# Key norms from the diagonal of (Gram matrix times decays), once per layer, and another PSUM bank for one unit

## The chip, the cores and the metric

The kernel runs on one core of a Trainium2 chip. The metric is device time in microseconds (us) for one execution; lower is better. Engines are named as in the profile: PE is TensorE (matmuls; PEld its weight loads), DVE is VectorE, ACT is ScalarE, POOL is GpSimd, and SP issues the DMAs. The times are a median of three runs; the profile is of one execution.

## The reference, cut to what matters

Two identical layers run on x, 512 tokens by 1024 features. In each, one projection feeds a gated DeltaNet branch (8 heads of 128) and a sliding-window attention branch (16 query heads of 64); both are merged, projected, and an MLP follows. Everything is float32. Of the DeltaNet branch the change concerns this:

```python
def l2norm(t):
    return t * lax.rsqrt(jnp.sum(t * t, axis=-1, keepdims=True) + EPS)      # EPS = 1e-6

k = l2norm(k.reshape(B, S, 8, 128)); beta = jax.nn.sigmoid(b_in); g = cumsum(g) in a chunk
decay = where(causal, exp(g[..., :, None] - g[..., None, :]), 0)
L = where(strict, einsum('bhnid,bhnjd->bhnij', k * beta[..., None], k) * decay, 0)
u = triangular_solve(L, v * beta[..., None], lower=True, unit_diagonal=True)
w = triangular_solve(L, k * beta[..., None] * exp(g)[..., None], lower=True, unit_diagonal=True)
a_intra = einsum('bhnid,bhnjd->bhnij', q, k) * decay
k_dec = k * exp(g_last - g)[..., None]
# then a scan over the chunks with the state S
```

So each key needs its squared norm (plus EPS): the inverse square root scales values, its inverse times beta scales the matrix that is solved, the intra-chunk products and the decayed keys. The decay matrix has ones on its diagonal.

## The kernel before, in words

**Weights and big matmuls.** PE is almost wholly taken up by weight matmuls. A float32 weight chunk of 128x1024 (`wr`, loaded by SP into 5 rotating buffers) is split into a high part `wh` (a cast on ACT, L323) and the rest `wl` (a subtraction on DVE, L324), up to 4 chunks ahead of PE. A chunk gives 24 matmuls of 128x512 output (`h_h,wh`, `h_l,wh`, `h_h,wl`; L339 to L341). The Tile scheduler orders the instructions of each engine from the program's dependences and its own estimates, except where the program fixes an order (`Order`, `keep_in_program_order`); an edit can therefore move work that it does not name.

**PSUM banks.** `PM` gives 2 banks for results of big matmuls (`ps_kp`, `ps_gb`, `ps_zp`, `ps_us` and so on), `PS` 3 banks for smaller results (`ps_s`, `ps_pt`, `ps_o`, `ps_gt`), `PK` one bank (Gram matrices `ps_a`, later `ps_i`), `PZ` two.

**Decays.** `decays()` transposes the cumulative log decays `gc` (128x32: partition = place in the chunk, column = head and chunk) on PE (`ps_gt`, L683), stores them in DRAM (`gd`) and broadcasts them into a 128x512 matrix `D` per head, which goes to DRAM (`dd`).

**The K stage** (16 rounds of the list `MIX`, about 80 to 190 us of the span in layer 1 and 986 to 1096 us in layer 2). Each round mixes big-matmul units (`gb_unit`: a merge gate; `ga_early`; `k_unit`: one head's keys) with one attention group of 128 queries by 4 heads. An attention group goes: scores `ps_s` on PE (L892, L893); mask add into `M`, maximum `nm`, `es`, and denominator `den` on DVE (L896 to L913); exponential and scaling of `M` on ACT (scaling L916); transposes `ps_pt` of `M` on PE (L922, bound to wait for L916); on DVE and POOL the high and low parts `pf_h`, `pf_l` (L412, POOL's mask `pc` L932); `ps_o` on PE (L938); the result into `qt` (L942).

`k_unit(h)` takes a key projection `ps_kp` through convolution and SiLU on DVE and ACT (`kk`, L714 to L718), loads `D`, and computes four 128x128 Gram matrices into `ps_a` (L735). Then DVE reads that bank twice: four operations with the identity (L740) that also sum each row into `ssk` (the squared norms), EPS (L742), the inverse root `irk` on POOL (L744), reciprocal (L747), times beta into `cj` (L748), and four operations that write `uu` = Gram times `cj` times `D` (L752). `uu` goes to DRAM (`ud`, L754).

**The solve.** From MIX's last rounds on, `solve()` runs in steps (`steps(n)` in the code) on DVE beside other units. It loads the 128 diagonal blocks of 32x32 (8 heads of 16) from `ud` into `ub`, one block per partition (L783); 31 steps of a product and a sum (L798, L801) invert them into `pb`; the result goes through DRAM (`pd`, L804) to `Tc` and, transposed, `Pc`.

**The V, Z and attention-output stages** follow: `ps_qp`, `ps_vp`, `ps_zp` units, and at about 246 us the loop over `ps_us` (attention output; takes the split attention results `oT_h`, `oT_l`; evacuated by L1214 into `mb`). `d_load` (L993) loads the matrix of a head (`ur`) from `ud`; `d_inverse` builds 128-wide inverses from `ur`, `Tc`, `Pc` with small matmuls `ps_i` (L1013, L1018), whose operands `T`, `Pt` POOL clears and copies (L1048); `d_turn` makes `kds` from `cj`; `d_chain` scales by `cj` and `irk` (`aT` L1155, `vs` and `kd` L1162).

## Time and profile before

| what | us |
|---|---|
| median of 3 runs | 1830.95 (1829.16 to 1831.1) |
| the profiled execution's own time | 1830.59 |
| span of that execution's profile | 1828.6 |
| PE busy, share of the span | 1809.1, 99% |
| PE weight loads (PEld) busy | 1503.9, 82% |
| DVE busy | 1292.1, 71% |
| ACT busy | 940.9, 51% |
| POOL busy | 211.2, 12% |
| mean granted TensorE clock | 0.999 |

A profile line of a group reads: line, engine, operation, output<-input by the program's names, shapes, count | busy us in total, mean ns of one | idle us of the engine ahead of them, and what ended most of it. A line of the timeline reads: start in us, duration, engine, line, operation, shapes, and in square brackets the engine's idle time just before and what ended it (the releaser). A line of the waits reads: who waits for whom: us in total, times, longest. "x4" at a timeline line means four in a row, with their common duration. Starts of consecutive big matmuls lie 0.22 to 0.23 us apart although each lasts 0.39 us: they are pipelined. DVE is busy 91% of the time in the K stage, against 71% over the span.

### The profile page before, as it was taken

The numbers are of one execution on the slowest core, as the hardware profiler recorded it, in microseconds if no ns is written. First come the engines' busy times: TensorE is split into PE (matmuls) and PEld (weight loads), VectorE is DVE, ScalarE is ACT, GpSimd is POOL, SyncE is SP. The second block draws the span as 40 slices with busy tenths as digits, with TensorE's granted clock in tenths as the row PEclk, the third lists the DMA queues.
The fourth block names the chain that finished last, engine by engine and source line by source line (L and its number), as shares of the span: only waits on it lengthen the run. The fifth ranks groups of instructions, "written<-read, shape, count | busy, mean of one in ns | idle before, by whom it ended". The sixth has DMA issues, their size and how long they took to land.

```text
span 1828.6 us, 26748 instructions
## 1 busy us (share of the span) xinstructions
PE 1809.1 (99%) x9598; PEld 1503.9 (82%) x9598; DVE 1292.1 (71%) x2466; ACT 940.9 (51%) x1913; POOL 211.2 (12%) x386
## 2 busy tenths in 40 slices
PE   9999999999999999999999999999999999999998
PEld 8888778888788888888898887888887898888886
DVE  5499796887566758684556997968885568585934
ACT  6678742444434645544347877234444346554442
POOL 0322102221101000000003221022111010000000
PEclk9999999999999999999999999999999999999999
DMA  5633447554453363564245343485545534544631
GB/s 188 202 118 116 115 149 223 179 170 149 124 191 124 96 216 120 168 217 151 93 151 181 104 127 110 167 234 165 160 139 153 172 119 135 174 163 148 233 102 46
DMA packets 146422, 278.48 MB, mean 152 GB/s; under 512 B 33569, under 2 KB 66657, under 8 KB 146290
## 3 DMA queue, kind: packets, MB, share of 16 engines
q1 hardware_dynamic: 145778, 276.75, 47.4%
q8 instruction: 75, 1.23, 0.3%
q14 instruction: 57, 0.47, 0.1%
q0 software_dynamic: 512, 0.03, 0.0%
HBM read 239.38 MB, written 37.36 MB: 151 GB/s over the span
## 4 chain that ended last, share of the span: by engine, by line
PE 84%; DVE 6%; ACT 5%; DMA 3%; issue 1%; POOL 1%; SPq 0%; POOLq 0%; DVEq 0%; ACTq 0%
PE ps_f L340 6%; PE ps_f L339 6%; PE ps_f L341 6%; PE ps_p L402 3%; PE ps_p L404 3%; PE ps_p L400 3%; PE ps_b L388 3%; PE ps_b L387 3%; PE ps_b L389 3%; PE ps_vp L339 2%; PE ps_us L339 2%; PE ps_ud L339 2%; PE ps_vp L341 2%; PE ps_ud L341 2%; PE ps_ud L340 2%; PE ps_us L340 2%
## 5 line engine op out<-in xcount | busy, mean ns | idle before, releaser
L323 ACT CAST wh<-wr 128x1024 fp32r<-128x1024 f32 (+1 forms) x332 | 343.1, 1040 | 542.2 <-PE ps_f L340 145.8
L324 DVE TENSOR_TENSOR wl<-wr,wh 128x1024 fp32r<-128x1024 f32 (+1 forms) x332 | 400.4, 1216 | 303.6 <-ACT wh L323 300.6
L339 PE MATMUL ps_f<-g_h,wh 128*128 128x512 f32 x448 | 174.3, 389 | 0.0
L340 PE MATMUL ps_f<-g_l,wh 128*128 128x512 f32 x448 | 174.3, 389 | 0.0
L341 PE MATMUL ps_f<-g_h,wl 128*128 128x512 f32 x448 | 174.3, 389 | 0.0
L402 PE MATMUL ps_p<-wl,P_h 128*128 128x512 f32 x336 | 131.4, 391 | 0.4 <-DVE wl L324 0.3
L404 PE MATMUL ps_p<-wh,P_l 128*128 128x512 f32 x336 | 130.8, 389 | 0.0
L400 PE MATMUL ps_p<-wh,P_h 128*128 128x512 f32 x336 | 129.5, 389 | 0.0
L437 POOL TENSOR_TENSOR pr<-pq,pw 128x1 f32<-128x1 f32 x16 | 9.8, 613 | 807.6 <-DVE pq L436 807.6
L339 PEld LDWEIGHTS ps_f<-g_h,wh 128*128 128x128 f32 x448 | 84.1, 188 | 17.4
L341 PEld LDWEIGHTS ps_f<-g_h,wl 128*128 128x128 f32 x448 | 84.1, 188 | 17.4
L340 PEld LDWEIGHTS ps_f<-g_l,wh 128*128 128x128 f32 x448 | 84.1, 188 | 17.4
L402 PEld LDWEIGHTS ps_p<-wl,P_h 128*128 128x128 f32 x336 | 63.1, 188 | 15.8 <-DVE wl L324 2.4
L400 PEld LDWEIGHTS ps_p<-wh,P_h 128*128 128x128 f32 x336 | 63.1, 188 | 13.3
L404 PEld LDWEIGHTS ps_p<-wh,P_l 128*128 128x128 f32 x336 | 63.1, 188 | 12.8
L387 PE MATMUL ps_b<-wh,h_h 128*128 128x432 f32 (+1 forms) x192 | 71.1, 370 | 0.0
L388 PE MATMUL ps_b<-wl,h_h 128*128 128x432 f32 (+1 forms) x192 | 70.5, 367 | 0.3 <-DVE wl L324 0.3
L389 PE MATMUL ps_b<-wh,h_l 128*128 128x432 f32 (+1 forms) x192 | 70.2, 366 | 0.0
L293 DVE TENSOR_TENSOR wr<-wr 128x1024 f32<-128x1024 f32 x48 | 58.0, 1220 | 2.6 <-DMA wr<-in_weights_dram 1.9
L340 PE MATMUL ps_qp<-h_l,wh 128*128 128x512 f32 x128 | 54.0, 422 | 0.0
L339 PE MATMUL ps_vp<-h_h,wh 128*128 128x512 f32 x128 | 53.9, 421 | 0.0
L341 PE MATMUL ps_vp<-h_h,wl 128*128 128x512 f32 x128 | 53.6, 419 | 0.0
(359 smaller groups left out, 4873.6 us busy)
## 6 DMA issues: line engine op xcount, KB each, us to landing
wr<-in_weights_dram SPq DMA_DIRECT2D x320, 512.0 KB, 3.5
wr<-in_weights_dram SPq DMA_DIRECT2D x24, 432.0 KB, 3.6
D<-dd SPq DMA_DIRECT2D x32, 256.0 KB, 3.2
xd<-xo SPq DMA_DIRECT2D x12, 512.0 KB, 2.8
xt<-xd SPq DMA_DIRECT2D x24, 256.0 KB, 3.7
D<-gd SPq DMA_DIRECT2D x16, 256.0 KB, 6.5
dd<-D SPq DMA_DIRECT2D x16, 256.0 KB, 3.9
kkd<-kk SPq DMA_DIRECT2D x16, 256.0 KB, 2.0
```

Of the source, the lines that this page charges most:

```text
L293: tt(out=held[j], in0=held[j], in1=part(i, k, j), op=ALU.add)
L323: nc.scalar.copy(wh[:, :w], wr[:, :w])
L324: sub(out=wl[:, :w], in0=wr[:, :w], in1=wh[:, :w].bitcast(F32), op=ALU.subtract)
L339: mm(ps, lhsT=wh[:, k, :], rhs=hi, start=k == 0, stop=False)
L340: mm(ps, lhsT=wh[:, k, :], rhs=lo, start=False, stop=False)
L341: mm(ps, lhsT=wl[:, k, :], rhs=hi, start=False, stop=k == KT - 1)
L387: mm(pss[t], lhsT=hi[:, tsl], rhs=wh[:, r, :], start=k == 0, stop=False)
L388: mm(pss[t], lhsT=hi[:, tsl], rhs=wl[:, r, :], start=False, stop=False)
L389: mm(pss[t], lhsT=lo[:, tsl], rhs=wh[:, r, :], start=False, stop=k == KT - 1)
L400: mm(pss[t], lhsT=hi[:, c], rhs=wh[:, r, :], start=first, stop=False, skip_group_check=onto)
L402: mm(pss[t], lhsT=hi[:, c], rhs=wl[:, r, :], start=False, stop=False, skip_group_check=onto)
L404: mm(pss[t], lhsT=lo[:, c], rhs=wh[:, r, :], start=False, stop=last, skip_group_check=onto)
```

## The change

`k_unit` reads the Gram bank once: `uu` = Gram times `D` in a single 128x512 product (L741 after), without norms. Since `D`'s diagonal is one, the squared norms stand on the diagonal of `uu`. `solve()` reads them from the diagonals of all its blocks at once: `ssq` = diagonal of `ub` plus EPS (L782, 128x32), sent to DRAM (`nd`), reciprocal, times beta in block layout (`bq`, loaded from the new `bd`), and one 128x1024 product scales `ub` (L786). `nd` comes back as `nT` (32x128); behind the last step a PE transpose `ps_nt` brings the norms to token layout, from which one reciprocal and one product make `cj` for all heads and POOL makes `irk` in one 128x32 power. `d_load` now scales `ur`, which is loaded unscaled, by `cj`: 4 activations of 128x128 per head on ACT. The transpose `ps_gt` carries beta along (64 columns rather than 32). And the first `ps_us` unit takes a bank of `PS` rather than `PM`.

Line numbers after the change are 2 to 8 higher (L323 becomes L325, L324 L326, L735 L739, L892 L897, L916 L921, L922 L927, L1214 L1222).

```diff
-        beta = s1("beta", 32)
+        gcb = s1("gcb", 64)
+        gc, beta = gcb[:, 0:32], gcb[:, 32:64]
...
             ps = PS("ps_gt")
-            tr(ps[:32, :P], gc, ident)
-            gT = sm.tile([32, P], F32, name="gT", bufs=1)
-            nc.vector.tensor_copy(gT, ps[:32, :P])
-            dma(gd, gT)
+            tr(ps[:64, :P], gcb, ident)
+            gT = sm.tile([64, P], F32, name="gT", bufs=1)
+            nc.vector.tensor_copy(gT, ps[:64, :P])
+            dma(gd, gT[0:32])
+            dma(bd, gT[32:64])
...
-        cj, irk = [], []
+        irk, cj = s1("irk", 32), s1("cj", 32)
...
             u_ = T[5]("uu")
-            sk_ = sm.tile([P, NC], F32, name="ssk")
-            for c in range(NC):
-                sl = slice(c * P, (c + 1) * P)
-                stt(out=u_[:, sl], in0=ps[:, sl], scalar=1.0, in1=ident, op0=ALU.mult,
-                    op1=ALU.mult, accum_out=sk_[:, c:c + 1])
-            ts(out=sk_, in0=sk_, scalar1=EPS, scalar2=None, op0=ALU.add)
-            ir = sm.tile([P, NC], F32, name="irk", bufs=H + 1)
-            ptt(out=ir, in0=sk_, in1=phalf, op=ALU.pow)
-            irk.append(ir)
-            cc = sm.tile([P, NC], F32, name="cj", bufs=H + 1)
-            nc.vector.reciprocal(cc, sk_)
-            tt(out=cc, in0=cc, in1=hc(beta)[:, h, :], op=ALU.mult)
-            cj.append(cc)
-            for c in range(NC):
-                sl = slice(c * P, (c + 1) * P)
-                stt(out=u_[:, sl], in0=ps[:, sl], scalar=cc[:, c:c + 1], in1=d[:, sl],
-                    op0=ALU.mult, op1=ALU.mult)
+            tt(out=u_, in0=ps, in1=d, op=ALU.mult)
             dma(umat(h), c4(u_))
...
+            bq = s1("bq", 32)
+            dma(bq, bd.rearrange("g (b j) -> (g b) j", b=4))
             pb = X4("pb")
...
             uv = ub.rearrange("p (j i) -> p j i", j=32)
+            sq = s1("ssq", 32)
+            ts(out=sq, in0=ub[:, 0:1024:33], scalar1=EPS, scalar2=None, op0=ALU.add)
+            dma(nd.rearrange("g (b j) -> (g b) j", b=4), sq)
+            nc.vector.reciprocal(sq, sq)
+            tt(out=sq, in0=sq, in1=bq, op=ALU.mult)
+            tt(out=uv, in0=uv, in1=sq.unsqueeze(2).broadcast_to([P, 32, 32]), op=ALU.mult)
+            nT = sm.tile([64, P], F32, name="gT", bufs=1)
+            dma(nT[0:32], nd)
...
+            ps = PS("ps_nt")
+            tr(ps[:, 0:32], nT[0:32], ident[:32, :32])
+            nc.vector.tensor_copy(irk, ps[:, 0:32])
+            nc.vector.reciprocal(cj, irk)
+            tt(out=cj, in0=cj, in1=beta, op=ALU.mult)
+            ptt(out=hc(irk), in0=hc(irk), in1=phalf.unsqueeze(1).broadcast_to([P, H, NC]), op=ALU.pow)
             dma(pd, pb)
...
                     dma(uview(h), umat(h))
+                    for c in range(NC):
+                        act(out=uview(h)[:, c, :], in_=uview(h)[:, c, :], func=AF.Copy,
+                            scale=cj[:, h * NC + c:h * NC + c + 1])
...
         for m in range(KT):
-            ps = PM("ps_us")
+            ps = (PM if m else PS)("ps_us")
```

(`d_turn` and `d_chain` take their columns from the two new tiles.) Instructions in the whole program: PE 8748 to 8750, DVE 2404 to 2258, ACT 1723 to 1787, POOL 391 to 377, SP 836 to 844.

The diff moves more than it names. PE's order stays the same outside the K stages, but there small blocks stand up to 16 big matmuls earlier: among the transposes `ps_pt` of layer 1, the third stands behind 402 big matmuls rather than 407, the tenth behind 572 rather than 585, the thirteenth behind 658 rather than 674, the last three where they were. PE, layer 1, where the second head's Gram matrices come, before:

```order
L340 MATMUL ps_gb<-h_l,wh 128x512
L341 MATMUL ps_gb<-h_h,wl 128x512
L892 MATMUL ps_s<-kT_h,qT 128x128
L735 MATMUL ps_a<-kk 128x128 x4
L938 MATMUL ps_o<-pf_l,vp 128x512
L893 MATMUL ps_s<-kT_l,qT 128x128
L892 MATMUL ps_s<-kT_h,qT 128x128
L893 MATMUL ps_s<-kT_l,qT 128x128
```

PE, the same place, after:

```order
L342 MATMUL ps_gb<-h_l,wh 128x512
L343 MATMUL ps_gb<-h_h,wl 128x512
L943 MATMUL ps_o<-pf_l,vp 128x512
L739 MATMUL ps_a<-kk 128x128 x4
L897 MATMUL ps_s<-kT_h,qT 128x128
L898 MATMUL ps_s<-kT_l,qT 128x128
L897 MATMUL ps_s<-kT_h,qT 128x128
L898 MATMUL ps_s<-kT_l,qT 128x128
```

The second half of one attention group (`ps_o`) now stands ahead of the Gram matrices, and all score matmuls of the next stand behind them.

DVE, about the first two heads of layer 1, before (`kk` and `qT` belong to key convolution and query layout):

```order
L747 RECIPROCAL cj<-ssk 128x4
L866 SCALAR_TENSOR_TENSOR qT<-ps_q,qT 64x512
L718 SCALAR_TENSOR_TENSOR kk<-th,kk 128x512
L748 TENSOR_TENSOR cj<-cj,beta 128x4
L896 TENSOR_TENSOR M<-ps_s,ban 128x256
L752 SCALAR_TENSOR_TENSOR uu<-ps_a,cj,D 128x128 x4
L896 TENSOR_TENSOR M<-ps_s,ban 128x256
L412 TENSOR_TENSOR pf_l<-ps_pt,pf_h 128x512
L904 TENSOR_REDUCE nm<-M 128x4
```

DVE, the same place, after:

```order
L871 SCALAR_TENSOR_TENSOR qT<-ps_q,qT 64x512
L718 SCALAR_TENSOR_TENSOR kk<-ps_kp,cw,kk 128x511
L901 TENSOR_TENSOR M<-ps_s,ban 128x256 x2
L722 SCALAR_TENSOR_TENSOR kk<-th,kk 128x512
L909 TENSOR_REDUCE nm<-M 128x4
L414 TENSOR_TENSOR pf_l<-ps_pt,pf_h 128x512
L910 TENSOR_TENSOR nm<-nm,nsk 128x4
L912 TENSOR_TENSOR es<-nm,nsk 128x4
L326 TENSOR_TENSOR wl<-wr,wh 128x1024
L741 TENSOR_TENSOR uu<-ps_a,D 128x512
```

The norm chain between the mask adds is gone; one product stands behind the next `wl`.

DVE at the start of the solve, layer 1, before (`oT_l` are split attention results):

```order
L324 TENSOR_TENSOR wl<-wr,wh 128x1024
L904 TENSOR_REDUCE nm<-M 128x4
L942 TENSOR_TENSOR qt_421<-ps_o,qt_421 64x512
L905 TENSOR_TENSOR nm<-nm,nsk 128x4
L412 TENSOR_TENSOR oT_l<-qt_419,oT_h 128x128
L907 TENSOR_TENSOR es<-nm,nsk 128x4
L412 TENSOR_TENSOR oT_l<-qt_420,oT_h 128x128
L324 TENSOR_TENSOR wl<-wr,wh 128x1024
L798 TENSOR_TENSOR tmp<-ub,pb 128x1
```

DVE, the same place, after:

```order
L912 TENSOR_TENSOR es<-nm,nsk 128x4
L782 TENSOR_SCALAR ssq<-ub 128x32
L414 TENSOR_TENSOR oT_l<-qt_421,oT_h 128x128
L414 TENSOR_TENSOR oT_l<-qt_422,oT_h 128x128
L917 TENSOR_TENSOR den<-den,es 128x4
L918 RECIPROCAL den<-den 128x4
L414 TENSOR_TENSOR oT_l<-qt_423,oT_h 128x128
L784 RECIPROCAL ssq<-ssq 128x32
L785 TENSOR_TENSOR ssq<-ssq,bq 128x32
L786 TENSOR_TENSOR ub<-ub,ssq 128x1024
L326 TENSOR_TENSOR wl<-wr,wh 128x1024
L797 TENSOR_TENSOR tmp<-ub,pb 128x1
```

The first read of `ub` (L782) now stands ahead of a softmax denominator (`den`), where the first step's product used to stand behind it.

ACT, behind the Z stage of layer 1, before:

```order
L1103 ACTIVATE sz<-ps_zp 128x512
L1111 ACTIVATE wq<-qq 128x512
L323 CAST wh<-wr 128x1024 x9
L772 ACTIVATE sga<-ps_ga 128x512
L323 CAST wh<-wr 128x1024
L772 ACTIVATE sga<-ps_ga 128x512
L1162 ACTIVATE vs<-kvx,irk 128x128
```

ACT, the same place, after:

```order
L325 CAST wh<-wr 128x1024
L1119 ACTIVATE wq<-qq 128x512
L325 CAST wh<-wr 128x1024 x7
L1000 ACTIVATE ur<-ur,cj 128x128 x15
L325 CAST wh<-wr 128x1024
L760 ACTIVATE sga<-ps_ga 128x512
L1000 ACTIVATE ur<-ur,cj 128x128
L325 CAST wh<-wr 128x1024
```

Fifteen scalings of `ur` stand between two casts; eight more come for heads 4 and 5 behind a later convolution, then four and two and two.

## The prediction

> **What bounds the kernel now.** I began with the engines' shares on the page, then took the K stages apart by windows, then asked what PE waited for in them, and last read the timeline around each wait.

> ```profile
> span 1828.6 us, 26748 instructions
> ...
> PE 1809.1 (99%) x9598; PEld 1503.9 (82%) x9598; DVE 1292.1 (71%) x2466; ACT 940.9 (51%) x1913; POOL 211.2 (12%) x386
> ```

> PE is busy in all but 1828.6 - 1809.1 = 19.5 us. A matmul's record overlaps the next one, so this alone proves little; but the starts of big matmuls below lie 0.22 to 0.23 us apart, one after another. Now the stretches that the change touches (K stage of layer 1, its end, K stage of layer 2):

> ```profile
> core 0: us, PE busy (x) PEld busy (x) DVE busy (x) ACT busy (x) POOL busy (x), PEclk, DMA share, GB/s
> 80.00:190.00 110.00, 108.14 (x573) 88.08 (x571) 100.03 (x296) 86.85 (x257) 26.78 (x46) 1.00 0.36 115
> 190.00:246.00 56.00, 55.30 (x263) 44.11 (x262) 44.53 (x122) 41.21 (x123) 7.55 (x12) 1.00 0.36 101
> 986.00:1096.00 110.00, 107.79 (x575) 88.23 (x573) 99.61 (x296) 86.52 (x257) 26.69 (x46) 1.00 0.36 115
> ```

> DVE is busy for 100.03 of 110 us, and still PE stands idle for only 110 - 108.14 = 1.9 us of them. What PE waited for from 80 to 250 us:

> ```profile
> PE ps_pt L922 <- ACT M L916: 2.0, 3, 0.8
> PE ps_us L339 <- DVE qq L714: 0.3, 1, 0.3
> PE ps_a L735 <- DVE uu L752: 0.2, 1, 0.2
> PE ps_o L938 <- POOL pc L932: 0.2, 1, 0.2
> ```

> That is 2.7 us a layer, and no relief of DVE can return more than the part of it that hangs on DVE. So whatever the change takes from DVE is mostly idle time given to DVE.

> **The Gram units.** Each of the 16 units of both layers loses four L740, four L752 and small column operations, and gains one 128x512 product of a PSUM bank with `D`.

> ```profile
> L740 DVE SCALAR_TENSOR_TENSOR uu<-ps_a,ident 128x128 f32<-128x128 f32 x64 | 16.1, 282 | 1.7 <-PE ps_a L735 0.8 <-issue 0.8
> L752 DVE SCALAR_TENSOR_TENSOR uu<-ps_a,cj,D 128x128 f32<-128x128 f32 x64 | 17.8, 340 | 0.1
> L1214 DVE SCALAR_TENSOR_TENSOR mb<-sgb,ps_us 128x512 f32<-128x512 f32 x16 | 10.9, 682 | 9.5 <-PE ps_us L341 9.5
> ```

> The product is priced by L1214, also a bank times an SBUF tile: 0.68. Relief: (16.1 + 17.8) / 16 - 0.68 = 1.4 us a unit, up to 1.7 with the small operations: 11.5 to 14 us of DVE a layer. What of it reaches PE I work out at the waits themselves:

> ```profile
> 88.67 0.66 PE L922 MATMUL ps_pt<-ident,M 128*128 128x128 f32 x4 [0.72 <-ACT M L916]
> ...
> 101.13 1.16 PE L735 MATMUL ps_a<-kk 128*128 128x128 f32 x8 [0.22 <-DVE uu L752]
> ...
> 107.06 0.66 PE L922 MATMUL ps_pt<-ident,M 128*128 128x128 f32 x4 [0.75 <-ACT M L916]
> ```

> ```profile
> 105.73 1.28 ACT L916 ACTIVATE M<-M,den 128x128 f32<-128x128 f32 x4 [0.59 <-DVE cj L747]
> ```

> The first wait (0.72) lies ahead of any Gram work: it stays. The second Gram unit's wait for the bank (0.22) goes: one read frees it rather than eight. The wait at 107.06 I expect to stay: the new order brings this transpose 5 big matmuls forward, 5 x 0.23 = 1.15 us, and PE comes 0.22 earlier besides; `M`'s scaling, which came at 105.73 behind DVE's norm work, gains about one unit's relief, 1.4. The two cancel, and I book 0 for these two waits together: -0.2 for the bank, +0.2 for an order that asks a little sooner than data come.

> ```profile
> 202.05 0.66 PE L922 MATMUL ps_pt<-ident,M 128*128 128x128 f32 x4 [0.51 <-ACT M L916]
> ```

> The wait at 202.05 (0.51) comes after all eight units, where DVE has gained most: I take it as gone, -0.5. For what PE's shorter gaps elsewhere in the stage may give (`ps_o` behind `pc`, 0.2) I book -0.3. Sum -0.8 a layer, -1.6 for both. Bounds: all waits but the first gone, -(2.7 - 0.72) = -2.0, and another -1.0 in gaps that the list of waits does not name (PE's idle time in the two windows, 1.9 + 0.7, is no more than those 2.7, so -3.0 in all is generous); the other way, the up to 16 matmuls (16 x 0.23 = 3.7 us) by which the order asks sooner for a transpose, less DVE's relief, leave PE standing: +1.8.

> **The bank of the first `ps_us`.**

> ```profile
> 245.35 0.39 PE L340 MATMUL ps_zp<-h_l,wh 128*128 128x512 f32 x1
> 245.57 0.39 PE L341 MATMUL ps_zp<-h_h,wl 128*128 128x512 f32 x1
> 246.25 0.47 PE L339 MATMUL ps_us<-oT_h,wh 128*128 128x512 f32 x1 [0.28 <-DVE qq L714]
> ```

> This unit waits until DVE has read the `PM` bank of two units before (`qq`). In a `PS` bank, free by then since the attention groups are over, it starts at the plain distance: (246.25 - 245.57) - (245.57 - 245.35) = 0.46 saved a layer, and its first record is 0.08 longer than 0.39. I take -0.5, -1.0 for both layers; the other end is 0, if the wait comes back at the second `ps_us`, which keeps its `PM` bank; that is 24 matmuls, 5.5 us, later, so I don't expect it.

> **The PE work added.** `ps_nt` is one more transpose, `ps_gt` a wider one. The like of it:

> ```profile
> 43.25 0.35 PE L388 MATMUL ps_b<-wl,h_h 128*128 128x432 f32 x1
> 43.44 0.27 PE L683 MATMUL ps_gt<-ident,gc 128*32 128x128 f32 x1
> ...
> 43.75 0.36 PE L387 MATMUL ps_b<-wh,h_h 128*128 128x432 f32 x1
> ```

> From 43.25 to 43.75 there are two big matmuls and the transpose; at 0.2 for each of these matmuls 0.1 is left for it. +0.12 a layer, +0.25 in all (0.1 to 0.5, since it has to wait for nothing: its input lies ready for 80 us).

> **The solve's new head.** DVE now reads `ub` (L782) ahead of group 13's `den`, and scales it in a 128x1024 product.

> ```profile
> 190.78 0.37 SPq L754 DMA_DIRECT2D ud<-uu  x1
> 193.13 0.36 SPq L783 DMA_DIRECT2D ub<-ud  x1
> ```

> ```profile
> 199.41 0.15 DVE L798 TENSOR_TENSOR tmp<-ub,pb 128x1 f32<-128x1 f32 x1
> ...
> 200.26 0.17 DVE L913 RECIPROCAL den<-den 128x4 f32<-128x4 f32 x1
> ```

> ```profile
> L324 DVE TENSOR_TENSOR wl<-wr,wh 128x1024 fp32r<-128x1024 f32 x308 | 375.5, 1229 | 259.0 <-ACT wh L323 256.2 <-PE ps_pt L922 2.3
> ```

> `ub` was there at 199.41 at the latest, 6.28 us behind its issue; `den` was done at 200.43. Behind L782 stand about 0.95 us of work up to that `den`, so nothing is late if `ub` lands by 199.4; with the last `uu` 1.4 us and more ahead, it lands by 198. The product costs like L324, 1.23, and delays the next mask and `wl` by that; PE has up to four split chunks in hand (24 x 0.23 = 5.5 us each). +0.2 a layer, +0.4 (0 to 1 a layer).

> Two rows show what POOL can add here:

> ```profile
> 204.28 0.64 POOL L932 TENSOR_SCALAR_AFFINE_SELECT pc<-pf_l 128x512 fp32r<-128x512 f32 x1 [0.20 <-DVE nm L905]
> 204.32 0.60 DVE L907 TENSOR_TENSOR es<-nm,nsk 128x4 f32<-128x4 f32 x1
> ```

> A column product of 128x4 took 0.60, ending with POOL's operation, where a 128x1 product took 0.15 (199.41). [...]

> **ACT, POOL and the queues.** `ur` takes 32 activations of 128x128 a layer, POOL one power of 128x32.

> ```profile
> L1162 ACT ACTIVATE vs<-kvx,irk 128x128 f32<-128x128 f32 x64 | 25.0, 390 | 3.5 <-DMA kvx<-vxd 3.5
> ```

> ```profile
> 289.84 1.05 ACT L323 CAST wh<-wr 128x1024 fp32r<-128x1024 f32 x1 [4.38 <-PE ps_us L340]
> 295.28 1.06 ACT L323 CAST wh<-wr 128x1024 fp32r<-128x1024 f32 x1 [4.38 <-PE ps_ga L340]
> ...
> 300.84 0.21 PE L1018 MATMUL ps_i<-Tc,ur 32*32 32x32 f32 x1
> ```

> By L1162 a scaling takes 0.39, fifteen 5.9 us. ACT idles 4.38 between two casts, so the cast at 295.28 starts some 1.5 to 3 us late; it works three chunks (16 us) ahead of PE: 0. The last of the fifteen ends by about 297.5, ahead of 300.84 by 3: 0. Without these covers, each us beyond 300.84 would be one for PE.

> ```profile
> L744 POOL TENSOR_TENSOR irk<-ssk,pw 128x4 f32<-128x4 f32 x16 | 18.1, 1129 | 109.7 <-DVE ssk L742 107.3 <-DVE den L913 2.3
> L437 POOL TENSOR_TENSOR pr<-pq,pw 128x1 f32<-128x1 f32 x16 | 9.8, 613 | 807.6 <-DVE pq L436 807.6
> ```

> ```profile
> 286.47 0.99 POOL L1048 MEMSET Pt<- 128x512 f32 x2 [36.41 <-PE ps_us L340]
> ```

> ```profile
> 304.88 0.53 PE L1013 MATMUL ps_i<-T,ur 64*64 64x64 f32 x6
> ```

> From 128x1 to 128x4 a power grows by (1.129 - 0.613) / 3 = 0.17 a column; 32 columns take 1.13 + 28 x 0.17 = 5.9 (1.1 if only the start counts, 9.0 if eight times L744). It stands behind the two clearings, so from 288.5 to 294.4; the copies into `T` come behind it, and PE reads `T` at 304.88: 0. The eight L744 off the K stage gain POOL nothing that PE waits for. The extra DMAs (`bd`, `nd`, `nT`, `bq`, four small ones a layer) stand on SP between weight loads that run chunks ahead; `nd` waits for L782 and holds the `wr` behind it at most the 1 to 2 us by which `ub` lands late: 0.

> **Sum** against the profiled execution's 1830.59 (0.36 under the median of the runs, 1830.95): -1.6 - 1.0 + 0.25 + 0.4 = -1.95, so 1828.6 there and 1829.0 against the median. About 0.2%, or 3.7 us, is what a measurement of this kernel can tell from no change; the forecast lies inside.

> **Rivals.** (1) *The stage's waits go and PE closes up*: -3.0 a layer, with the bank -1.0 in all: 1830.95 - 7 + 0.65 = 1824.6. For it: the share of 91% on DVE. Against: the list of waits has only 2.0 a layer behind Gram work. Chance 0.28.

> (2) *DVE is the bound in the K stage.* Its relief of 11.5 to 14 us a layer comes out at the end, 1830.95 - 2 x 12.6 = 1805.7, if PE has as much slack as its weight loads show (88.08 of 110, 22 us free). [...] Against is this row:

> ```profile
> L339 PEld LDWEIGHTS ps_f<-g_h,wh 128*128 128x128 f32 x448 | 84.1, 188 | 17.4
> ```

> A load of 0.188 in each plain distance of 0.22 to 0.23 makes 82 to 85%, with no matmul ever waiting: at this share there is no room. Chance 0.03.

> (3) *`ub` lands late, slower.* Its load now stands ahead of `den`, so each us beyond 199.4 is a us for the transpose behind it. From 6.28 us behind the issue it decides; at 3 us more in each layer the time is 1829.0 + 6 = 1835. For it: SP's `ub` waits for `ud` to be written (190.78 to 193.13), and PE comes sooner. Chance 0.12.

> (4) *The order outruns its data*, the +1.8 a layer of the Gram part instead of -0.8: 1829.0 + 5.2 = 1834.2, on the edge of what can be told. Chance 0.08.

> My forecast (waits partly gone) has 0.49. **Chances**: faster by over 0.2% (below 1827.3) takes (1), (2) and a little of mine: 0.33; slower (above 1834.6) most of (3) and half of (4): 0.14; same 0.53. **Range**: up into (4), 1833.5; down past (1) with its gaps a little larger, 1823.5.

> **What would show it.** Right: `uu` a single record of about 0.68; DVE below 90 us in the first window with PE still near 108; `ps_us` at 0.23 behind `ps_zp`; no wait at the transpose near 202; the casts after 290 late with no PE wait behind. Wrong: PE waiting for `den`, `M` or `wl` after 190 (3), transposes waiting longer between 110 and 190 (4), or fewer PE idle us than 2.7 minus 2.0 a layer (1), or a stage shorter by ten us (2).

## The result, and the profile after

The change made the kernel slower: 1835.1 us, median of 8 runs (1834.06 to 1837.09), against 1830.45 us before (8 runs, 1829.16 to 1831.55). The ratio is 1.0027, 95% interval 1.0016 to 1.0038, so +4.65 us. The prediction said 1829.0 within 1823.5 to 1833.5: it missed on the slow side, less than 1 us from the total of its fourth rival (1834.2), though not by that rival's mechanism. The profiled execution took 1835.97 us with a span of 1834.2, 5.6 above the span before.

The page's engines, then the windows of the prediction with one more, short one:

```profile
PE 1811.1 (99%) x9600; PEld 1506.4 (82%) x9600; DVE 1276.4 (70%) x2256; ACT 960.9 (52%) x1977; POOL 205.9 (11%) x372
```

```profile
core 0: us, PE busy (x) PEld busy (x) DVE busy (x) ACT busy (x) POOL busy (x), PEclk, DMA share, GB/s
80.00:190.00 110.00, 106.06 (x559) 87.07 (x558) 90.42 (x187) 85.73 (x253) 19.66 (x40) 0.98 0.35 112
190.00:246.00 56.00, 55.15 (x262) 43.64 (x261) 41.86 (x119) 41.91 (x124) 7.07 (x10) 1.00 0.34 94
986.00:1096.00 110.00, 106.06 (x566) 87.04 (x565) 91.30 (x186) 86.38 (x256) 21.73 (x44) 1.00 0.36 113
158.00:162.40 4.40, 4.40 (x19) 3.88 (x18) 3.02 (x8) 1.71 (x5) 0.00 (x0) 0.61 0.47 164
```

DVE's busy time in the first window fell from 100.03 to 90.42, as the change meant it to. PE's fell too, from 108.14 to 106.06 (in layer 2 from 107.79 to 106.06): PE stood idle for 2.1 us more. The 56 us behind it hardly differ (55.30, now 55.15). And for 4.4 us from 158.0 PE worked at a granted clock of 0.61, which costs 4.4 x 0.39 = 1.7 us. What PE waited for from 80 to 250 us, and the places:

```profile
PE ps_o L943 <- POOL pc L937: 2.4, 2, 1.9
PE ps_pt L927 <- ACT M L921: 1.1, 2, 0.7
PE ps_o L943 <- DVE pf_l L414: 1.0, 3, 0.6
```

```profile
100.88 0.50 PE L943 MATMUL ps_o<-pf_l,vp 128*128 128x512 f32 x1 [0.57 <-DVE pf_l L414]
...
105.32 0.65 PE L927 MATMUL ps_pt<-ident,M 128*128 128x128 f32 x4 [0.33 <-ACT M L921]
...
157.59 0.50 PE L943 MATMUL ps_o<-pc,vp 128*128 128x512 f32 x1 [1.90 <-POOL pc L937]
...
1066.91 0.50 PE L943 MATMUL ps_o<-pc,vp 128*128 128x512 f32 x1 [1.91 <-POOL pc L937]
```

The waits of the transposes for `M` shrank from 2.0 to 1.1, and that for `ps_a`'s bank is gone. A new one is larger than both: the second half of attention group 7 waits 1.9 us (2.06 from start to start, beyond the plain distance) for POOL's second mask `pc`, in both layers. POOL at that time:

```profile
151.61 0.64 POOL L937 TENSOR_SCALAR_AFFINE_SELECT pc<-pf_h 128x512 fp32r<-128x512 f32 x1 [6.61 <-ACT pf_h L413]
152.21 0.46 POOL L831 TENSOR_TENSOR rt<-qt,cs 128x128 f32<-128x128 f32 x1
...
153.05 0.90 POOL L833 TENSOR_TENSOR rt<-qt,cs 128x128 f32<-128x128 f32 x1
...
154.70 1.19 POOL L833 TENSOR_TENSOR rt<-kv,cs 128x16 f32<-128x16 f32 x1
...
156.85 0.68 POOL L937 TENSOR_SCALAR_AFFINE_SELECT pc<-pf_l 128x512 fp32r<-128x512 f32 x1
```

Ten of the twelve rotary operations of the fourth query block (`rt`, `qt`) stand between the two masks of group 7, though nobody needs that block for four more groups. In the kernel before, two stood there, behind a root `irk`, and the mask started at 154.35:

```profile
152.22 1.01 POOL L744 TENSOR_TENSOR irk<-ssk,pw 128x4 f32<-128x4 f32 x1
153.19 0.46 POOL L826 TENSOR_TENSOR rt<-qt,cs 128x128 f32<-128x128 f32 x1
153.61 0.47 POOL L827 TENSOR_TENSOR rt<-qt,cs 128x128 f32<-128x128 f32 x1
154.35 0.64 POOL L932 TENSOR_SCALAR_AFFINE_SELECT pc<-pf_l 128x512 fp32r<-128x512 f32 x1 [0.27 <-DVE pf_l L412]
```

For the experiments I use the length of the K stage, from the start of the first `ps_kp` matmul to the start of the first `ps_vp` matmul of a layer; in between every kernel here has the same 763 matmul records. Before, it is 149.28 and 149.14 us (layers 1 and 2), after, 152.83 and 151.67: +3.55 and +2.53. Elsewhere the change gives 0.45 a layer at `ps_us` and takes 0.34 a layer at `ps_nt`, and the stretch from `ps_vp` to `ps_zp` is 0.4 longer a layer (its mask `pc` is late; in a second profile of the same kernel only layer 2's is longer).

### The profile page after: what moved, and what is told of

It is laid out like the page before. It is cut to its first block, busy times and chain, and to the rows that moved or that the text cites. A ratio compares the mean times of both kernels' runs of the same rounds, so it can differ in the third digit from the quotient of the medians.

```text
span 1834.2 us, 26607 instructions
## 1 busy us (share of the span) xinstructions
PE 1811.1 (99%) x9600; PEld 1506.4 (82%) x9600; DVE 1276.4 (70%) x2256; ACT 960.9 (52%) x1977; POOL 205.9 (11%) x372
## 4 chain that ended last, share of the span: by engine, by line
PE 84%; DVE 7%; ACT 4%; DMA 3%; POOL 1%; issue 1%; SPq 0%; DVEq 0%; POOLq 0%; ACTq 0%
PE ps_f L342 6%; PE ps_f L341 6%; PE ps_f L343 5%; PE ps_p L404 3%; PE ps_p L406 3%; PE ps_p L402 3%; PE ps_b L390 3%; PE ps_b L389 3%; PE ps_b L391 3%; PE ps_vp L341 2%; PE ps_us L341 2%; PE ps_ud L341 2%; PE ps_vp L343 2%; PE ps_us L342 2%; PE ps_us L343 2%; PE ps_ud L343 2%
## 5 line engine op out<-in xcount | busy, mean ns | idle before, releaser
L325 ACT CAST wh<-wr 128x1024 fp32r<-128x1024 f32 (+1 forms) x332 | 343.5, 1041 | 518.6 <-PE ps_f L342 145.9
L326 DVE TENSOR_TENSOR wl<-wr,wh 128x1024 fp32r<-128x1024 f32 (+1 forms) x332 | 401.0, 1219 | 305.5 <-ACT wh L325 300.6
L341 PE MATMUL ps_f<-g_h,wh 128*128 128x512 f32 x448 | 174.3, 389 | 0.0
L341 PEld LDWEIGHTS ps_f<-g_h,wh 128*128 128x128 f32 x448 | 84.1, 188 | 17.5
L342 PEld LDWEIGHTS ps_f<-g_l,wh 128*128 128x128 f32 x448 | 84.1, 188 | 17.4
L343 PEld LDWEIGHTS ps_f<-g_h,wl 128*128 128x128 f32 x448 | 84.1, 188 | 17.4
L404 PEld LDWEIGHTS ps_p<-wl,P_h 128*128 128x128 f32 x336 | 63.1, 188 | 16.1 <-DVE wl L326 2.7
L915 ACT ACTIVATE M<-M,nm 128x128 f32<-128x128 f32 x128 | 49.8, 391 | 12.3 <-DVE nm L910 12.3
L341 PE MATMUL ps_vp<-h_h,wh 128*128 128x512 f32 x128 | 53.9, 421 | 0.0
```

The source lines that it names most:

```text
L325: nc.scalar.copy(wh[:, :w], wr[:, :w])
L326: sub(out=wl[:, :w], in0=wr[:, :w], in1=wh[:, :w].bitcast(F32), op=ALU.subtract)
L341: mm(ps, lhsT=wh[:, k, :], rhs=hi, start=k == 0, stop=False)
L342: mm(ps, lhsT=wh[:, k, :], rhs=lo, start=False, stop=False)
L343: mm(ps, lhsT=wl[:, k, :], rhs=hi, start=False, stop=k == KT - 1)
L404: mm(pss[t], lhsT=hi[:, c], rhs=wl[:, r, :], start=False, stop=False, skip_group_check=onto)
```

## The experiments

Theories: (A) POOL's queue; (B, C) the new order of PE in the K stage as a whole, with DVE's relief as a gain that it hides; (D) DVE's relief is worth nothing to PE; (J, K) the Gram units or the solve's head. The other letters are explained where a run was expected by them. All ratios are to the kernel before on the same chip.

| kernel | K stage 1, 2 (us) | ratio, 95% interval |
|---|---|---|
| before | 149.28, 149.14 | 1 |
| after | 152.83, 151.67 | 1.0027 [1.0016, 1.0038] |
| after_again | 152.98, 152.27 | 1.0034 [1.0021, 1.0048] |
| held | 149.89, 150.94 | 1.0015 [1.0006, 1.0024] |
| before_rotary_ahead | 152.60, 150.95 | 1.0028 [1.0017, 1.0039] |
| before_root_off_pool | 153.95, 153.48 | 1.0053 [1.0040, 1.0065] |
| bank_alone | 149.27, 149.20 | 0.9995 [0.9986, 1.0005] |
| after_old_pe_order | 153.97, 152.10 | 1.0054 [1.0042, 1.0067] |
| after_old_order_held | 153.98, 153.77 | 1.0070 [1.0057, 1.0082] |
| before_new_pe_order | 158.81, 160.39 | 1.0125 [1.0111, 1.0138] |
| after_all_old_orders | 153.30, 154.38 | 1.0051 [1.0038, 1.0063] |
| after_old_orders_den_first | 153.64, 153.57 | 1.0045 [1.0032, 1.0058] |
| before_all_new_orders | 166.19, 164.63 | 1.0180 [1.0166, 1.0194] |
| k_units_alone | 150.95, 151.13 | 1.0032 [1.0020, 1.0045] |
| solve_part_alone | 149.67, 149.68 | 1.0006 [0.9997, 1.0015] |
| old_orders_row_scale | 153.45, 153.20 | 1.0045 [1.0032, 1.0057] |
| old_orders_solve_late | 149.33, 149.16 | 1.0105 [1.0089, 1.0120] |

**held.**

```diff
             if (g, e) == (1, 0) and t < NT - 1:
                 att_rope(t + 1)
+                # t == 2: its POOL operations ordered behind the last pc issued
```

> The changed kernel, with one edit to POOL's order: the rotary work of the fourth block of 128 queries is held until the last mask of the group two ahead is issued, so the second mask pc of attention group 7 no longer stands behind ten rotary operations. The orders of DVE, ACT and SP are those of the changed kernel, PE's differs in four rows at that place. Theory A (POOL's queue: the mask comes 2.06 us late in each layer, and in layer 1 PE then runs 4.4 us at a granted clock of 0.61, which costs 2.6 more): both waits and the low clock go, 1835.1 - 2 x 2.07 - 2.6 = 1828.4, faster than before by 2. Theory B (the whole new order of the K stage asks too early, this wait is one of many): PE meets the next late operand instead and half or less comes back, 1832 to 1835.

The wait of 2.06 fell to 1.06, the low clock was gone, and the K stages were 2.94 and 0.73 shorter than after. That settles that POOL's queue was a cause, but not the only one: theory A's 1828.4 did not come (its 2.6 for the low clock was also too much; 1.7 is right), and the total, 1.0015 x 1830.45 = 1833.2, lies in theory B's 1832 to 1835. The rest of the wait has another cause, in the rows of DVE and POOL:

```profile
155.43 1.22 DVE L326 TENSOR_TENSOR wl<-wr,wh 128x1024 fp32r<-128x1024 f32 x1
```

```profile
155.58 1.56 POOL L943 TENSOR_SCALAR_AFFINE_SELECT pc<-pf_l 128x512 fp32r<-128x512 f32 x1 [2.46 <-DVE pf_l L414]
```

The mask took 1.56 rather than 0.64, and ended 0.49 behind the end of a `wl` subtraction on DVE; at 0.64 it would have been done 0.92 earlier, which is the whole wait. So too in the changed kernel: its three longest masks, 1.20 us at 127.21 and 1036.54 and 1.21 at 1110.56, each ran beside a `wl` subtraction for 0.7 us, while 38 of its 48 took 0.63 or 0.64.

**before_rotary_ahead**, the converse: the old kernel with the rotary work between the masks.

```diff
                     pvs.append((at["v", t], 256, b))
+                    # group 7: att_rope(3) behind the first pc, the second pc behind ten of its operations
```

> The kernel before, with one edit to POOL's order: the rotary work of the fourth block stands between the two masks of attention group 7, as it does after the change. The other engines keep their orders but for one row each on PE and ACT. Theory A: the mask starts when the rotary work ends, about 157.5 rather than 154.4, and PE waits some 2.5 to 3 us in each layer: 1830.5 + 5 to 6 = 1835.5 to 1836.5, and up to 2 x 2.6 more where the clock then falls as in layer 1 of the changed kernel. Theory B (PE's matmuls behind the mask don't hold up the big ones): under 1 us in all, 1830.5 to 1831.5.

```profile
157.91 0.50 PE L952 MATMUL ps_o<-pc,vp 128*128 128x512 f32 x1 [1.81 <-POOL pc L932]
```

PE waited 1.8 us for the mask (2.3 in layer 2), the K stages grew by 3.3 and 1.8, and the total by 5 us: with nothing else of the change, about the loss of the change. In layer 1 a stretch at a low clock followed (0.57 from 158.5 to 162.5), in layer 2 none. The waits and their price are shown.

**before_root_off_pool.**

```diff
-            ptt(out=ir, in0=sk_, in1=phalf, op=ALU.pow)
+            nc.vector.reciprocal(ir, sk_)
```

> The kernel before, with the eight roots irk per layer replaced by a reciprocal on DVE (the values' scale is then the inverse square rather than the inverse norm; nothing else is left out). Nothing else of the change is in it. Theory A (taking the root off POOL lets the scheduler put the rotary work ahead of the mask): a wait of PE on the mask pc of about 2 us appears in each layer near 157 and 1066 us, with or without a stretch at low clock: 1830.5 + 4 to 7 = 1834.5 to 1837.5. Theory B (the fall comes from the solve's new head, the scaling of ur, the added transposes, or DVE's shorter queue): no such wait, 1829.5 to 1831.5.

The scheduler did put the rotary work between two masks, here all twelve operations, but PE waited for no mask in the K stage: POOL was through at 159.41 and then stood idle for 1.58 us until DVE had `pf_l`. The scheduler also moved much on PE, DVE and ACT, and the loss was 4.5 us a layer; the waits for `pf_l` (1.1), `M` (2.2) and `ps_a` (0.5) account for a part of it. Theory A has the order right, but neither the wait nor the size; theory B misses both. It shows that eight operations of 1 us taken from POOL, with eight of 0.17 us added on DVE, can through the new order cost twice what the change cost.

**bank_alone.**

```diff
-            ps = PM("ps_us")
+            ps = (PM if m else PS)("ps_us")
```

> The kernel before, with the first ps_us unit in a bank of PS rather than PM, and nothing else. As predicted: PE's wait for qq at 246.25 and 1152.70 goes and with it 0.46 a layer, 1830.5 - 0.9 = 1829.6. Rival: the wait comes back at the next unit that takes a PM bank: 1830.5.

The stretch from `ps_zp` to `ps_us` is 5.44 us in both layers, against 5.89 before: 0.45 a layer, as predicted. The total, 0.9995, can't tell 0.9 from nothing.

**after_old_pe_order, after_old_order_held, before_new_pe_order.** A list fixes PE's order in the K stage:

```diff
+        on_pe = [i_ for i_ in nc.cur_bb.bb.instructions[k_first:] if i_.engine == nc.tensor.engine]
+        for a_, b_ in zip(PE_ORDER, PE_ORDER[1:]):
+            # ordering dependence of on_pe[b_] on on_pe[a_]
```

> The changed kernel with PE held, in the K stage, to the order that PE has in the kernel before (a list of the 772 instructions of a layer, as ordering dependences); the other engines' orders are the scheduler's. POOL's queue still has the rotary work ahead of masks of group 7, now ahead of both. Stage length from the first ps_kp to the first ps_vp was 149.28 and 149.14 us before, 152.83 and 151.66 after. Theory C (the new PE order is what costs; DVE's relief itself is worth 1.8 us a layer, seen as ps_pt behind M falling from 2.9 to 1.4 and ps_a's wait of 0.3 gone): stage lengths 147.5 plus what the rotary work still costs, 0 to 2; total 0.9978 to 1.000 of the kernel before. Theory D (DVE's relief is worth nothing to PE in any order): stage 149 to 151, total 1.000 to 1.002.

> As the run before it, and the rotary work of the fourth block held behind the masks of group 8 as well. PE's order is the same. Theory C: stages of 147.3 to 147.7, so -3.5 for both layers, with the bank's -0.9 and +0.7 that the stretch behind the attention output has gained in the changed kernel: -3.7 us, 0.998 of the kernel before. Theory D: stages of 149 to 150, total 0.9995 to 1.001.

> The kernel before with PE held, in the K stage, to the order that PE has after the change; everything else is the scheduler's, and DVE has its old work. Theory C (order costs, relief gives back): what the changed kernel loses plus the relief that it has and this one lacks, stage 153 to 155 a layer, total +7 to +11 us, 1.004 to 1.006 of the kernel before. Theory D (relief worth nothing): stage 151.5 to 153 as after the change, +5 us, 1.003. Theory E (POOL's queue alone is what costs; PE's order is harmless): stage 149 to 150.5, under 1.0015.

With PE's old order the changed kernel was slower than with its new one, and no better with the rotary work held (layer 2's stage is 1.7 longer, the totals' intervals overlap): theory C falls, and theory D's numbers too. PE waited 3.2 us for `M` and 1.3 for `pf_h` where the other queues, ordered anew by the scheduler, were now behind PE's old order. The old arithmetic in PE's new order lost 9.5 and 11.3 us a layer. An order of one queue is good or bad only with those of the others.

**after_again.** The changed kernel, unedited.

> The changed kernel once more, unchanged, on the chip of the other three, for a second profile. Theory F (a wait of PE of some 2 us may be followed by a stretch at a lower granted clock, in some executions or layers and not in others): the waits on the mask pc of 2.06 and 2.07 us are there again, the stretch of 4.4 us at 0.61 behind the first of them is there or not, and the K stages are 151.7 where it is missing and 152.8 where it is there. Theory G (the stretch belongs to the place): it is behind the first wait again and not behind the second. Total 1.0027 of the kernel before.

The waits on `pc` were there again, 1.91 in both layers. The stretch at 0.61 was there behind the first (158.5 to 162.9) and missing behind the second, as theory G has it. But the place alone does not decide: k_units_alone, below, had the same two waits and no such stretch. The last section shows how the waits lay.

**after_all_old_orders, after_old_orders_den_first, before_all_new_orders.** The list now covers all five queues, from the K stage to the end of the attention output; where a kernel has operations of its own, these are free or, in a Gram unit, stand in the other's place.

```diff
+        for e_, want in FIXED.items():      # tensor, vector, scalar, gpsimd, sync
+            # ordering dependences along want, the other kernel's order
```

> The changed kernel with all five queues (PE, DVE, ACT, POOL, SP) held, from the K stage to the end of the attention output, to the order of the kernel before; the product that makes uu stands where the first of the four L740 stood. Operations that only the changed kernel has are free. Holding PE's order alone had made it slower still, with transposes waiting 3.3 us for M, so only the orders together can tell what DVE's shorter work is worth. Theory H (the change costs through the new orders of all queues, and its lighter DVE work is worth something in the old ones): K stages of 147.3 to 148.3 a layer against 149.2 before, less up to 1 for the scaling of ub ahead of den; total 0.998 to 0.9995 of the kernel before. Theory D (DVE's relief is worth nothing to PE): K stages 149 to 150 and the total 0.9998 to 1.001.

> As the run before it, with two edits to the solve's head: group 13's den and its reciprocal stand ahead of the scaling of ub, and the reciprocal of ssq goes to a tile of its own, so that it doesn't wait for the DMA that reads ssq (1.45 us of DVE in the changed kernel's profile at 200.12). Theory H: 0.3 to 0.7 us a layer below the run before it, total 0.9975 to 0.999 of the kernel before. Theory D: as the run before it, 0.9998 to 1.001.

> The kernel before with all five queues held, over the same stretch, to the order of the changed kernel; the eleven DVE operations of a Gram unit stand where the one product of the changed kernel stands, and POOL's roots are free. Theory H (new orders cost, the lighter work gives back a part): worse than the changed kernel, K stages of 154 to 157 against its 151.7 to 152.8, total 1.004 to 1.008 of the kernel before. Theory D: K stages of 151.5 to 153, as in the changed kernel, total 1.003.

In the first, PE came to 190 us as the kernel before did, 113.19 us behind its first `ps_kp` against 113.18, and then, in layer 1, lost all at one place, the solve's head:

```profile
200.60 0.35 DVE L876 RECIPROCAL ssq<-ssq 128x32 f32<-128x32 f32 x1 [0.82 <-DMA nd<-ssq]
...
201.21 1.22 DVE L878 TENSOR_TENSOR ub<-ub,ssq 128x1024 f32<-128x1024 f32 x1
...
203.40 0.17 DVE L1010 RECIPROCAL den<-den 128x4 f32<-128x4 f32 x1
```

```profile
205.00 1.11 PE L1019 MATMUL ps_pt<-ident,M 128*128 128x128 f32 x4 [3.27 <-ACT M L1013]
```

The reciprocal works in place, so it waits for the DMA that reads `ssq`; with the product behind it, `den` is 3.1 us later than before (203.40 against 200.26) and the transpose waits 3.27, followed by a stretch at a low clock (0.64 from 205.0 to 209.4). With `den` first the loss moved to `pf_l` (2.58 a layer). Both theories' totals were missed; before 190 us, D is right. The old arithmetic in all the new orders lost 16.9 and 15.5 us a layer: of the two, the new orders fit the light Gram units alone.

**k_units_alone and solve_part_alone** divide the change.

```diff
 k_units_alone:    +  stt(out=u_, in0=ps, scalar=1e-4, in1=d, op0=ALU.mult, op1=ALU.mult)   # and no norms anywhere
 solve_part_alone: +  ssq, nd, reciprocal, product on ub (by ones), ps_nt, POOL's power     # in the kernel before
```

> The change's Gram units alone: one product of bank and decays a unit (with a constant 0.0001 in it), no norms on DVE or POOL, and nothing in their place: no scaling of ub, no transpose of norms, no scaling of ur, constants for cj and irk, the old bank for ps_us. The scheduler gives PE nearly the order of the changed kernel in the K stage. Theory J (the lighter units alone make the scheduler choose the new orders, and these cost): the rotary work stands ahead of the mask, K stages of 151.5 to 153, 1.002 to 1.0035 of the kernel before. Theory K (the solve's head is what costs): K stages of 147.5 to 149.5, 0.998 to 1.000.

> The kernel before with the change's solve part added as idle work: the diagonal of ub plus EPS, its way through DRAM, the reciprocal, the 128x1024 product on ub (by ones), the transpose ps_nt, the small products and POOL's power of 128x32. The Gram units are the old ones. The scheduler keeps PE's old order but for a few rows at the end of the K stage, and puts den ahead of the reciprocal that waits for the DMA. Theory J: K stages of 149 to 150 and +0.34 a layer for ps_nt, 1.000 to 1.001. Theory K: K stages of 151 to 154, 1.002 to 1.005.

This is theory J, with K stages a little shorter than it said. The Gram units alone bring the wait of 1.9 us on `pc` in each layer, K stages 1.7 and 2.0 longer, and 1.0032 (some 6 us, of which the K stages explain 3.7; the rest lies outside them and is not traced to a cause); the solve part alone, in the scheduler's hands, adds 0.4 and 0.5 to the K stages and can't be told from no change.

**old_orders_row_scale and old_orders_solve_late** ask once more what DVE's relief is worth, with the solve's head out of the way.

```diff
-            tt(out=uv, in0=uv, in1=sq.unsqueeze(2).broadcast_to([P, 32, 32]), op=ALU.mult)
...
-                    tt(out=tv, in0=uv[...], in1=pv[...], op=ALU.mult)
+                    stt(out=tv, in0=uv[...], scalar=sr[:, j:j + 1], in1=pv[...], op0=ALU.mult, op1=ALU.mult)
 old_orders_solve_late: the first 13 steps behind group 14's result in DVE's list
```

> All five queues held to the order of the kernel before, den ahead of the solve as in the run with den first, and the 128x1024 product on ub left out: each step's product takes the row's factor as its scalar instead. The solve's head is then some 0.5 us of DVE rather than 1.8, its steps start about 1 us later than before instead of 3. Theory L (in the old orders DVE's relief is worth nothing to PE; all the loss there was the head standing ahead of den and pf_l): pf_l's wait at 207 falls from 2.6 to 0.3 to 1, without a stretch at low clock, K stages of 149.3 to 150.2; total 0.9998 to 1.0008. Theory M (relief is worth about 1 a layer once the head is gone): K stages of 148 to 148.7, 0.9985 to 0.9995.

> As the run before it, and the first 13 steps of the solve stand behind group 14's result on DVE, so that nothing of the solve stands between den, M and pf_l of groups 13 and 14. Theory L: waits for M and pf_l as in the kernel before or a little shorter, K stages of 148.6 to 149.3, total -0.9 for the bank, +0.7 for ps_nt, -0.5 for the shorter waits at 202: 0.9992 to 1.0000. Theory M: K stages of 147.5 to 148.3, 0.998 to 0.999. If the solve then ends too late, a wait for Tc or ur appears near 300 us.

In the first, `pf_l` was still 2.2 late, because the solve's steps that stand ahead of it start behind `den`; both theories missed that. The second answers the question. Its window, and the two records that bound its K stage:

```profile
80.00:190.00 110.00, 107.42 (x574) 87.70 (x572) 89.68 (x187) 86.82 (x258) 16.90 (x38) 1.00 0.37 117
```

```profile
76.79 0.48 PE L433 MATMUL ps_kp<-h_h,wh 128*128 128x512 f32 x1
...
226.12 0.48 PE L433 MATMUL ps_vp<-h_h,wh 128*128 128x512 f32 x1
```

DVE had 10.35 us less to do in this window than before, all orders were the old ones, and the K stage took 226.12 - 76.79 = 149.33 us, against 149.28: over the stage, the relief is worth nothing to PE. It was worth something in between. At the second Gram unit, whose bank came free sooner, PE got 0.38 ahead of the kernel before, and by 157 us, in layer 1, it was 0.95 ahead; then it lost most of that at one new wait, and the rest behind it:

```profile
157.67 0.36 PE L990 MATMUL ps_s<-kT_h,qT 128*128 128x256 f32 x1 [0.72 <-DVE M L998]
```

DVE could not use its free time there: where its norm operations had stood, it now waited 2.34 us, up to 154.87, for a cast of `vp` in ACT's queue.

(Behind the K stage I had put the steps ahead of group 15's `pf_l`, where PE then waited 6.3 us and ran at half clock for 6.8 us behind (10.2 in layer 2); the stretch from `ps_vp` to `ps_zp` grew by 8.3 and 9.2 us, which is nearly all of this kernel's loss, and theory L's total missed it.)

## Why the prediction was wrong, step by step

**Which step failed.** The K stages were forecast 0.6 us a layer shorter (-0.8 for the Gram units, +0.2 for the solve's head) and came out 3.55 and 2.53 longer; no other term is off by more than 0.5 a layer. The prediction priced the new orders at +0.2, for PE's queue, and at nothing for POOL's. The runs showed in its place a wait of 2.06 us for a mask in each layer and, behind it in layer 1, a half clock that cost 1.7.

**The Gram units: the gain.** The reason given for the gain failed too: "`M`'s scaling ... gains about one unit's relief, 1.4", and with it the -0.5 at 202 and the -0.3 for small gaps. In the old orders `M` came no earlier, relative to PE: the wait of 0.75 at 107 became 0.90, and that at 202 stayed (0.59 in old_orders_solve_late). ACT's queue shows why. Before, then after_all_old_orders, whose first `ps_kp` is 0.17 later (the gate `sgb` is L763 before and L751 after the change):

```profile
100.66 1.05 ACT L323 CAST wh<-wr 128x1024 fp32r<-128x1024 f32 x1 [1.96 <-PE ps_gb L340]
101.73 0.60 ACT L763 ACTIVATE sgb<-ps_gb 128x512 f32<-128x512 f32 x1
102.59 0.58 ACT L941 COPY qt<-ps_o 64x512 f32<-64x512 f32 x1 [0.26 <-PE ps_o L938]
103.20 0.40 ACT L910 ACTIVATE M<-M,nm 128x128 f32<-128x128 f32 x1
```

```profile
102.52 0.58 ACT L1038 COPY qt<-ps_o 64x512 f32<-64x512 f32 x1
103.12 0.40 ACT L1007 ACTIVATE M<-M,nm 128x128 f32<-128x128 f32 x1
...
105.58 1.28 ACT L1013 ACTIVATE M<-M,den 128x128 f32<-128x128 f32 x4 [0.52 <-DVE den L1010]
```

The exponentials of `M` stand in ACT's queue behind a cast, a gate and a copy, which wait for PE's own matmuls (`ps_gb`, `ps_o`). The chain that PE waits for starts at PE, and DVE's norm operations filled a gap in it. I had read the last releaser, "DVE cj L747", as the cause of the delay. Only where the scheduler moved the copy and the gate behind the exponentials did the wait shrink, so it was not the relief alone that took `M`'s waits from 2.0 to 1.1. Nor was it the order alone: with the old arithmetic in the new orders (before_all_new_orders) they were 6.6. After the change:

```profile
101.24 0.39 ACT L915 ACTIVATE M<-M,nm 128x128 f32<-128x128 f32 x1
...
102.89 0.58 ACT L946 COPY qt<-ps_o 64x512 f32<-64x512 f32 x1
103.50 0.60 ACT L751 ACTIVATE sgb<-ps_gb 128x512 f32<-128x512 f32 x1
103.99 1.27 ACT L921 ACTIVATE M<-M,den 128x128 f32<-128x128 f32 x4
```

The scaling starts at 103.99 rather than 105.73, with the first exponential at 101.24 rather than 103.20. Counted from the first `ps_kp` (76.42 and 76.94) the scaling is 1.2 earlier, where 1.4 was forecast, and the wait at 202 is gone as forecast: these numbers came by luck, since the reason given for them, the relief by itself, does not hold.

**The order: the loss.** I let "the eight L744 off the K stage gain POOL nothing that PE waits for" stand for the whole of POOL's queue. That is the step that cost the forecast: without the roots the rotary work moved ahead of a mask, for 2.06 us a layer. The rival "the order outruns its data" (+1.8 a layer, a total of 1834.2, chance 0.08) came near the total by luck: it had PE's order asking too soon for transposes in mind, and no transpose waited between 110 and 190. What came was a late mask, and +3.55 and +2.53, of which 1.7 in layer 1 is the low clock, for which the prediction had no term.

**The bank** was right: 0.46 forecast, 0.45 measured a layer, with `ps_us` at the plain distance:

```profile
249.02 0.39 PE L343 MATMUL ps_zp<-h_h,wl 128*128 128x512 f32 x1
249.24 0.39 PE L341 MATMUL ps_us<-oT_h,wh 128*128 128x512 f32 x1
```

**`ps_nt`** was mis-sized: 0.12 a layer forecast, 0.34 measured (the stretch from `ps_us` to `ps_i` went from 54.59 to 54.93). My row had a transpose between matmuls of 432 columns, at 0.1; here from 287.10 to 287.93 there are two big matmuls, 0.46, and the transpose costs the rest, 0.37:

```profile
287.10 0.39 PE L343 MATMUL ps_us<-oT_h,wl 128*128 128x512 f32 x1
287.42 0.24 PE L804 MATMUL ps_nt<-ident,gT 32*128 32x32 f32 x1
287.59 0.50 PE L341 MATMUL ps_us<-oT_h,wh 128*128 128x512 f32 x1
287.93 0.40 PE L342 MATMUL ps_us<-oT_l,wh 128*128 128x512 f32 x1
```

**The solve's head.** The late `ub` of rival (3) did not come; what came is a wait that I had missed, of the in-place reciprocal for the DMA that reads `ssq`:

```profile
196.99 0.18 DVE L782 TENSOR_SCALAR ssq<-ub 128x32 f32<-128x32 f32 x1
...
200.12 0.35 DVE L784 RECIPROCAL ssq<-ssq 128x32 f32<-128x32 f32 x1 [1.45 <-DMA nd<-ssq]
```

With `den` ahead of it in the scheduler's order it cost PE little: in solve_part_alone the K stages grew by 0.4 and 0.5, with +0.2 forecast and up to 1 allowed. Ahead of `den`, in after_all_old_orders, the whole head made PE wait 3.3 us in layer 1 rather than 0.5.

**What was hidden stayed hidden.** The product `uu` took 0.68 (forecast 0.68), the fifteen scalings of `ur` 4.50 us (5.9 forecast; 0.30 each, back to back) and the cast behind them came late at 298.75 with no PE wait behind, POOL's power 5.45 (5.9 forecast):

```profile
L741 DVE TENSOR_TENSOR uu<-ps_a,D 128x512 f32<-128x512 f32 x16 | 10.9, 683 | 1.2 <-PE ps_a L739 1.2
```

```profile
290.74 5.45 POOL L808 TENSOR_TENSOR irk<-irk,pw 128x32 f32<-128x32 f32 x1
...
294.35 4.50 ACT L1000 ACTIVATE ur<-ur,cj 128x128 f32<-128x128 f32 x15
298.75 1.03 ACT L325 CAST wh<-wr 128x1024 fp32r<-128x1024 f32 x1
```

The rival "DVE is the bound" fell: 10 us off DVE did not shorten the stage.

**What stays open**: why the scheduler's orders for the lighter units are worse than for the heavier ones (it works from its own estimates), and what decides whether a wait of PE is followed by the low clock (last section). The stretch from `ps_i` to the first `ps_ud` differed by up to 5 us between the profiles of these kernels (188.0 to 193.3), without a relation to the edits; so totals are less sharp than the K stages. No kernel here beat the kernel before beyond its interval.

## What to carry to other kernels

An engine that is 91% busy beside one that is 98% busy may still be worth nothing to it: before pricing relief, follow the chain that the waiting engine waits for back through every queue, and see whether it starts at that engine itself. Where a scheduler orders the queues, an edit's own work is the smaller part; read its new order on every engine, the idle ones above all, at each place where an operand of the bottleneck stands behind work that could wait. A tuned order belongs to its own durations on all queues together: holding one queue, or all of them around another arithmetic, made the total worse each time.

## What the runs showed of the hardware

```profile
155.33:158.74 3.41, 1.51 (x9) 1.19 (x8) 3.06 (x7) 1.23 (x5) 2.61 (x7) 1.00 0.51 159
158.74:162.16 3.42, 3.42 (x14) 3.02 (x13) 2.50 (x6) 0.88 (x4) 0.00 (x0) 0.50 0.33 111
1063.28:1066.69 3.41, 1.73 (x11) 1.38 (x10) 3.32 (x5) 1.98 (x6) 3.41 (x8) 1.00 0.33 103
1066.69:1070.11 3.42, 3.20 (x19) 2.85 (x20) 3.11 (x8) 1.45 (x5) 0.57 (x3) 1.00 0.53 206
```

In layer 1 the wait of 1.90 lies within one cell: PE is busy for only 1.51 us of it, and the next cell runs at 0.50. In layer 2 the end of a cell cuts the wait of 1.91 in two, 1.69 and 0.22, and the clock stays. So too in before_rotary_ahead: 1.60 busy, then half clock; in layer 2 a longer wait, 2.26, is cut into 1.30 and 0.96, and nothing follows. In k_units_alone the waits of 1.9 us are cut in both layers; the cells have 2.22 and 1.65 busy, and nothing follows. The same place of the program lay within one cell in layer 1 and across two in layer 2, so I take the 1.7 us as partly luck. No bound is shown: a cell with 1.63 us busy (205.18 in old_orders_row_scale) and one with 2.07 (95.31 in before_all_new_orders) were followed by half clock, one with 1.57 (1064.85 in after_old_order_held) was not.
